# Seven products on quarters in place of eight for the second FFN product, in three of its four parts

## The chip, the core and the metric

The kernel is one program on one NeuronCore of a Trainium2 chip. The metric is the device time of one execution in microseconds (us), taken as the median of several runs. Its engines are TensorE (PE in the profile; PEld is its weight load), VectorE (DVE), ScalarE (ACT), GpSimd (POOL) and SyncE (SP). Sixteen DMA engines move the data. SP starts plain loads, POOL starts loads that add to what is already in the on-chip memory.

## What is computed

Two layers, each a mixer block and a feed-forward block (FFN) on a sequence of 512 tokens of width 1024, all in fp32:

```python
for l in range(2):
    h = rms_norm(x, pre_mix_norm[l])
    ...                                   # conv, pooling, gated unit, sparse attention on h @ w_in
    x = x + rms_norm(mix @ w_out[l], post_mix_norm[l])
    h = rms_norm(x, pre_ffn_norm[l])
    f = square(relu(h @ ffn_w1[l]))       # 512x1024 @ 1024x4096
    x = x + rms_norm(f @ ffn_w2[l], post_ffn_norm[l])   # 512x4096 @ 4096x1024
```

The change lies in `f @ ffn_w2` and in what feeds it.

## The kernel before, in words

Every fp32 product is done as three fp32r matmuls (`mm3`): each operand is split into a high and a low part, and high x high, high x low and low x high are added up in PSUM. A weight unit is 128 x 1024 words (512 KB). `load` brings it from HBM into a raw buffer `wr` (six of them) through SP's queue; `split` makes the high part `wh` on ACT and the low part `wl` on DVE (five buffers each). Of a raw buffer in use, `more` adds another unit to it with an accumulating DMA from POOL, so that a sum of weights costs no engine but the DMA.

The FFN runs in four parts of 1024 hidden columns. In a part, `square4` is called twice. Each call makes a 512 x 512 block of `h @ ffn_w1` by seven products on quarters (Strassen's scheme, Winograd's form) of 24 matmuls with 256 columns each: the seven forms of h are held in `F`, four weight units are loaded, and four accumulating DMAs make the weight sums. `finish` applies the squared relu to a quarter and splits it into `f` (tiles `f`, `hi`, `lo`). Then `tgroup` runs the second product of the part twice, for the two halves of the 1024 output columns: four weight units, four token tiles, 96 matmuls of 512 columns each. The first half's sums go from PSUM (`pm`) into `y` in SBUF by one addition for each token tile; the second half's stay in four PSUM banks of their own (`own`, tile name `po`) over all four parts. After the last part come the norm (`square`, `post`) and the next layer's norm (`norm_tile`).

The order in which every engine works is not that of the text. The kernel is first recorded (`_Rec.add`), then `order` plays it through with a cost for each instruction, for DMA landing times and for free buffers, and each engine's fixed list follows from that; `shift` moves an instruction's rank. A tile of a pool is given out in the order of the text as far as buffers go. Pools that matter here: `wr` 6, `wp` 5, `sc` (scratch, 128 x 512 words) 9, `big` (8 KB a partition: forms `F`, `f`, `y`, mixer tiles) 12, and eight PSUM banks by tag: `mm` 3, `o` 1, `s` 2, `x` 2.

In the listing all instructions are issued from line 442, so the profile's rows tell them apart by the names of the tiles. The lines that the steps touch are `cost` and `order`, `conv_in`, `square4` (`finish`, `first`, the chain of `more`), `mixer`, `ffn` and `POOLS`.

Of the kernel before, what the change touches and what calls it, by code (L numbers as in the profile page):

```python
# [10 lines left out]
F32 = mybir.dt.float32  # L11
# [3 lines left out]
AF = mybir.ActivationFunctionType  # L15
# [4 lines left out]
P = 128  # L20
# [18 lines left out]
FIRST = (2, 3)  # L39
NBIG, NSC = 12, 9  # L40

# [189 lines left out]
class _Rec:  # L231
# [56 lines left out]
    def cost(self, eng, method, args, kw):  # L288
# [6 lines left out]
        if eng == "tensor":  # L295
            if method == "transpose":
                return 0.107
            dt, m = args[1].dtype, args[1].ix.size
            if out.p0:
                return 0.02  # L300
            if dt == F32:
                return max(4 * (n / 2400 + 0.0025), 0.426 * m / 128 if n < 128 else 0.0)
            if dt == F32R:
                return max((17 * n / 16 + 10) / 2400, 0.109 * m / 128)
            return max(0.025, n / 2400 + 0.0025)
# [21 lines left out]
    def order(self):  # L327
# [43 lines left out]
        while len(seq) < n:  # L371
# [30 lines left out]
            if o[1] == "dma_start":  # L402
                v = o[2][0] if isinstance(o[2][0], _V) else o[2][1]
                dma = max(dma, end + 1.1) + v.pn * v.ix.size * 4 / 360e3
                end = dma + (2.0 if e == "sync" else 4.0)
            for t in o[5]:
# [37 lines left out]

POST, FORM, FORM2, FORM3, C11 = -1000, -1000, 0, 500, 500


class _Net:
# [81 lines left out]
    def split_psum(self, hi, lo, ps, scale=None):  # L530
# [4 lines left out]
        else:  # L535
            self.act(hi, ps, AF.Copy, scale=scale)
            self.stt(lo, ps, scale, hi.bitcast(F32), ALU.mult, ALU.subtract)

    def grow(self, l, c0, n):
        t = self.gpool.tile([P, n], F32, name=self.nm("gb"), tag=f"gb{n}", bufs=2)  # L540
        r = self.a["rows"]
        self.nc.sync.dma_start(t, bass.AP(tensor=r.tensor, offset=r.offset + l * r.shape[1] + c0,
                                          ap=[[0, P], [1, n]]))
        return t
# [49 lines left out]
    def norm_forms(self, t, g, forms, tag="x"):  # L594
# [20 lines left out]
        def put(i, v):  # L615
            hi, lo = F[i][:, :, c:c + P], F[i][:, :, 256 + c:256 + c + P]
            self.split_psum(hi, lo, v)
# [9 lines left out]
        r0, r1 = raw[t - 2, 0], raw[t - 2, 1]  # L627
        s3, s1 = four("hs"), four("hs")
        self.act(s1, pts[1])
        self.tt(s1, s1, pts[0], ALU.subtract)  # L630
        put(3, s1)
        self.tt(s3, r0, pts[0], ALU.subtract)
        self.stt(r0, s1, -1.0, r0, ALU.mult, ALU.subtract)
        put(4, r0)
        self.nc.shift = FORM3
        put(5, s3)
        self.stt(r1, r0, -1.0, r1, ALU.mult, ALU.subtract)
# [85 lines left out]
    def conv_in(self, pv, pg, b):  # L723
        th = self.scr("th")
        self.act(th, pg, AF.Tanh, scale=0.5)
        h = self.mp.tile([P, 30 + S], F32, name=self.nm("ch"), tag="ch", bufs=2)
        self.nc.gpsimd.memset(h[:, :30], 0.0)
        self.stt(h[:, 30:], th, 1.0, pv, ALU.add, ALU.mult)
        return h
# [204 lines left out]
    def cmp_probs(self):  # L934
# [13 lines left out]
        self.tt(pc, pc, self.cmask[:, :, None, :].to_broadcast([P, NT, 4, 32]), ALU.add)  # L948
        st = self.mp.tile([P, 3, NT, 4], F32, name=self.nm("cst"), tag="cst", bufs=1)
        nc.vector.tensor_reduce(st[:, 0], pc, AX.X, ALU.max)  # L950
# [9 lines left out]
    def attn_tile(self, i, mix):  # L960
# [64 lines left out]
        nc.tensor.transpose(pt, self.pc[:, i].rearrange("p h n -> p (h n)"), self.ident)  # L1025
        th = self.mp.tile([P, P], F32, name=self.nm("pch"), tag="pch", bufs=1)
        self.act(th, pt)
# [121 lines left out]
    def new_norm(self, l, c0):  # L1149

        return self.grow(l, c0, D), self.new_hT()

    def square4(self, l, u, f, F, early=None):

# [20 lines left out]

        def out(bh, th):
            o = (slice(None), slice(2 * bh, 2 * bh + 2), slice(256 * th, 256 * th + 256))
            return f[0][o], f[1][o]

        def finish(c, op, bh, th):  # L1180
            hi, lo = out(bh, th)
            self.stt(c, c, 0.0, c, op, ALU.mult)
            self.act(hi, c)
            self.tt(lo, c, hi.bitcast(F32), ALU.subtract)

# [5 lines left out]
        def first():  # L1191
            w21 = self.split(self.load(l, u + 1))
            product(a, w21, A12)
            r = view(self.scr("fr"))
            hi, lo = out(0, 0)
            self.nc.shift = C11 if early is not None else 0
            self.act(r, a, AF.Relu)
            self.act(hi, r, AF.Square)
            self.tt(r, r, r, ALU.mult)
            self.tt(lo, r, hi.bitcast(F32), ALU.subtract)  # L1200
            self.nc.shift = 0
# [10 lines left out]
        if early is not None:  # L1212
            first()
            yield
        more(B11, 2)
        B12 = self.load(l, u + 2)
        more(B12, 3)
        t1 = self.split(B11)
        x = bank()
        product(x, t1, S1, True)  # L1220
        c = snap("c", x)
        more(B11, 3)
        t2 = self.split(B11)
        z = bank("o")
        product(z, t2, S2, True)
        add(s1, z)
        add(c, s1)
        more(B11, 1)
        if early is None:
            first()  # L1230
        t3 = self.split(B12)
        y = bank()
        product(y, t3, S3, True)
        add(c, y)
        finish(c, ALU.min, 1, 1)
        w22 = self.split(self.load(l, u + 3))
        product(x, w22, S4)
        c = view(self.scr("c"))
        self.tt(c, s1, x, ALU.add)
        finish(c, ALU.min, 1, 0)  # L1240
        t4 = self.split(B11)
        product(y, t4, A22)
# [4 lines left out]
    def mixer(self, l, norm):  # L1247
# [9 lines left out]
        self.KH, self.KL = K[:, 0:2], K[:, 2:4]  # L1257
        self.V = self.mp.tile([P, NT, P], F32, name=self.nm("V"), tag="V")
        self.Vc = self.mp.tile([P, 2, P], F32, name=self.nm("Vc"), tag="Vc")
        self.Kc = self.mp.tile([P, 64], F32R, name=self.nm("Kc"), tag="Kc")  # L1260
        st = {}

        def mixt():
            t = self.big("mixT")
            return t[:, 0:2], t[:, 2:4]
# [44 lines left out]
        def cout():  # L1310
            st["conv"] = mixt()
            self.conv_out(st["acc"], st["conv"])

        for name in ORDER:
# [5 lines left out]
        m = [(st[n][0][:, c], st[n][1][:, c]) for n in ("nsa", "pool", "sgu", "conv") for c in range(2)]  # L1320
        g = self.grow(l, 1024, D)
        ssv = self.small.tile([P, NT, 2], F32, name=self.nm("ssv"), tag="ssv", bufs=2)
# [3 lines left out]
        places = [self.big("wa") for _ in range(2)]  # L1326
        after = self.grow(l, 2048, D), self.new_forms()
        for dh in range(2):
# [17 lines left out]
    def ffn(self, l, norm):  # L1346
        (g, (F, _)), y = norm
        g2 = self.grow(l, 3072, D)
        after = None
        ssv = self.small.tile([P, NT, 2], F32, name=self.nm("ssv"), tag="ssv", bufs=2)  # L1350

        own = [self.pst([P, 512], "po", "x" if t < 2 else "s") for t in range(NT)]
        u0, n = U_FF, PART
        for part in range(NPART):
            f = [[self.big("f") for _ in range(2)] for _ in range(2)]
            both = [self.square4(l, u0 + 4 * i, (f[0][i], f[1][i]), F, y[:, i] if part == 0 else None)
                    for i in range(2)]
            if part == 0:
                for _ in range(2):
                    for s in both:  # L1360
                        next(s)
            for s in both:
                for _ in s:
                    pass
            u0 += n
            srcs = [(f[0][k // 4][:, k % 4], f[1][k // 4][:, k % 4]) for k in range(n)]
            end = part == NPART - 1
            for t, ps in self.tgroup(lambda j: self.unit(l, u0 + j), srcs, 2):
                yt = y[:, t]
                if part == 0:  # L1370
                    self.act(yt, ps)
                    continue
                self.tt(yt, ps, yt, ALU.add)
                if end:
                    self.square(yt, ssv[:, t, 0:1])
                    self.tt(yt, yt, g2[:, 0:512], ALU.mult)
            u0 += n // 2
            if end and l + 1 < L:
                after = self.new_norm(l + 1, 0)
            for t, ps in self.tgroup(lambda j: self.unit(l, u0 + j), srcs, n // 2 if end else 2, own, part == 0, end):  # L1380
                if not end:
                    continue
                yt = self.scr("yg")
                self.square(ps, ssv[:, t, 1:2], yt)
                self.tt(yt, ps, g2[:, 512:], ALU.mult)
                self.post(t, [y[:, t], yt], ssv[:, t])
                if after:
                    self.norm_tile(t, *after)
            u0 += n // 2
        return after  # L1390

    POOLS = (("cp", 1), ("small", 2), ("par", 1), ("gp", 2), ("sc", NSC), ("wp", 5), ("wr", 6), ("mp", 1),
             ("big", NBIG), ("psum", 2))

# [78 lines left out]
```

## Time and profile before

| | us |
|---|---|
| median of three runs (lowest, highest) | 1073.33 (1072.13, 1074.9) |
| the profiled execution, its own time | 1071.21 |
| its span, first to last instruction | 1069.5 |
| PE busy in the span | 1054.3 |
| DVE busy | 726.1 |
| ACT busy | 505.9 |
| POOL busy | 92.6 |
| time of the DMA packets, share of 16 engines | 28.5% from SP's queue, 19.2% from POOL's |

The profile is of one execution. A row of a group of instructions gives the engine, the operation, the tiles (out<-in), the shape, the count, the busy time, the mean duration of one in ns, and then the idle time of that engine before them with what ended it. Matmuls are pipelined, so the duration of one is longer than the distance from one to the next; distances are read from the chain of work. FFN parts begin where the chain goes over to tile `pf` (the first product).

### The profile page before, as it was taken

The numbers are of one execution on the slowest core, as the hardware profiler recorded it, in microseconds if no ns is written. First come the engines' busy times: TensorE is split into PE (matmuls) and PEld (weight loads), VectorE is DVE, ScalarE is ACT, GpSimd is POOL, SyncE is SP. The second block draws the span as 40 slices with busy tenths as digits, with TensorE's granted clock in tenths as the row PEclk, the third lists the DMA queues.
The fourth block names the chain that finished last, engine by engine and source line by source line (L and its number), as shares of the span: only waits on it lengthen the run. The fifth ranks groups of instructions, "written<-read, shape, count | busy, mean of one in ns | idle before, by whom it ended". The sixth has DMA issues, their size and how long they took to land.

```text
span 1069.5 us, 16960 instructions
## 1 busy us (share of the span) xinstructions
PE 1054.3 (99%) x6850; PEld 920.6 (86%) x6850; DVE 726.1 (68%) x1118; ACT 505.9 (47%) x893; POOL 92.6 (9%) x144
## 2 busy tenths in 40 slices
PE   8999999999999999999999999999999999999997
PEld 6998777898898898898899986788989988988986
DVE  7799876895276366277669998669924753752773
ACT  5437774763252253154444487648423523532531
POOL 3000001200100100100000000111000000001000
PEclk9999999999999999999999999999999999999999
DMA  9330216456566566467144111344665655656512
GB/s 338 106 120 21 79 43 154 110 131 202 119 177 177 97 180 187 91 154 231 38 131 137 60 54 42 64 119 118 178 144 115 175 165 131 172 162 137 155 46 79
DMA packets 39265, 137.44 MB, mean 129 GB/s; under 512 B 4753, under 2 KB 5649, under 8 KB 38930
## 3 DMA queue, kind: packets, MB, share of 16 engines
q1 hardware_dynamic: 29970, 102.79, 28.5%
q0 software_dynamic: 9216, 33.56, 19.2%
q8 instruction: 54, 0.88, 0.3%
q14 instruction: 25, 0.20, 0.1%
HBM read 134.23 MB, written 2.10 MB: 127 GB/s over the span
## 4 chain that ended last, share of the span: by engine, by line
PE 84%; DVE 12%; issue 1%; ACT 1%; POOL 1%; DMA 0%; DVEq 0%; POOLq 0%; SPq 0%; ACTq 0%
PE pf L442 28%; PE pm L442 23%; PE po L442 16%; PE pp L442 6%; PE pc L442 3%; DVE wl L442 3%; DVE cacc L442 2%; PE s L442 2%; PE O L442 2%; PE ppt L442 2%; PE pt L442 1%; DVE h L442 1%; DVE pw L442 1%; DVE xb L442 1%; DVE hs L442 0%
## 5 line engine op out<-in xcount | busy, mean ns | idle before, releaser
L442 DVE TENSOR_TENSOR wl<-wr,wh 128x1024 fp32r<-128x1024 f32 (+1 forms) x220 | 262.4, 1203 | 176.2 <-ACT wh L442 174.3
L442 ACT ACTIVATE wh<-wr 128x1024 fp32r<-128x1024 f32 (+1 forms) x222 | 227.9, 1042 | 275.8 <-DMA wr<-wst 89.6
L442 PE MATMUL pf<-hF,wh 128*128 128x256 f32 x1728 | 300.1, 278 | 1.4 <-DVE hF L442 0.8
L442 PEld LDWEIGHTS pf<-hF,wh 128*128 128x128 f32 x1728 | 262.5, 188 | 4.1 <-DVE hF L442 1.2
L442 PE MATMUL pf<-hF,wl 128*128 128x256 f32 x864 | 238.4, 278 | 0.1
L442 PEld LDWEIGHTS pf<-hF,wl 128*128 128x128 f32 x864 | 162.4, 188 | 1.7 <-DVE wl L442 0.8
L442 PE MATMUL pm<-wh,f 128*128 128x512 f32 x512 | 163.3, 395 | 0.0
L442 PE MATMUL po<-wh,f 128*128 128x512 f32 x512 | 160.5, 392 | 0.0
L442 PEld LDWEIGHTS pm<-wh,f 128*128 128x128 f32 x512 | 96.2, 188 | 23.5 <-DVE c L442 1.8
L442 PEld LDWEIGHTS po<-wh,f 128*128 128x128 f32 x512 | 96.2, 188 | 20.5
L442 POOL DMA_DIRECT2D wr<-wst x64 | 55.4, 866 | 560.1 <-DVE wl L442 404.1
L442 PE MATMUL po<-wl,f 128*128 128x512 f32 x256 | 100.5, 392 | 0.0
L442 PE MATMUL pm<-wl,f 128*128 128x512 f32 x256 | 100.2, 391 | 0.0
L442 PE MATMUL pp<-wh,hT 128*128 128x256 f32 (+1 forms) x512 | 100.2, 289 | 0.0
L442 DVE SCALAR_TENSOR_TENSOR cacc<-ch,cwh,cacc 128x512 f32<-128x512 f32 x120 | 85.1, 742 | 0.5
L442 PE MATMUL pm<-wh,mixT 128*128 128x512 f32 x256 | 83.7, 403 | 0.1
L442 PEld LDWEIGHTS pp<-wh,hT 128*128 128x128 f32 x512 | 80.0, 189 | 0.6
L442 PE MATMUL pp<-wl,hT 128*128 128x256 f32 (+1 forms) x256 | 73.6, 287 | 0.0
L442 PEld LDWEIGHTS pm<-wh,mixT 128*128 128x128 f32 x256 | 47.7, 189 | 12.1 <-issue 1.0
L442 PEld LDWEIGHTS po<-wl,f 128*128 128x128 f32 x256 | 48.1, 188 | 10.8
L442 PEld LDWEIGHTS pm<-wl,f 128*128 128x128 f32 x256 | 48.1, 188 | 9.3
L442 PE MATMUL pm<-wl,mixT 128*128 128x512 f32 x128 | 50.4, 396 | 0.0
(236 smaller groups left out, 1378.4 us busy)
## 6 DMA issues: line engine op xcount, KB each, us to landing
wr<-wst SPq DMA_DIRECT2D x170, 512.0 KB, 4.3
wr<-wst POOLq DMA_DIRECT2D x64, 512.0 KB, 5.8
gb<-rows SPq DMA_DIRECT2D x7, 512.0 KB, 4.9
wr<-wq SPq DMA_DIRECT2D x8, 268.0 KB, 4.6
xres<-x SPq DMA_DIRECT2D x4, 512.0 KB, 5.9
cw<-cw SPq DMA_DIRECT2D x2, 1024.0 KB, 8.1
out<-xres SPq DMA_DIRECT2D x3, 512.0 KB, 2.6
sgw<-sgw SPq DMA_DIRECT2D x2, 256.0 KB, 5.3
```

The source lines that it names most:

```text
L442: getattr(getattr(nc, e), method)(*[real(x) for x in args], **{k: real(x) for k, x in kw.items()})
```

## The change

In parts 0 to 2 the second product (512 x 1024 times 1024 x 1024) is done by seven products on quarters too: 256 tokens x 512 hidden columns times 512 x 512 weights, 24 matmuls of 512 columns each. `square4` no longer splits its result itself but hands each quarter to `emit`, which builds the left-hand forms A11, S3, A12, S1, S2, S4 and A22 (tile names as in `form`), each split in a high and a low part. The weight sums for p5, p7, p6 and q4 are made by accumulating DMAs on raw buffers, two chains of them starting from unit 0 and unit 4. Two of the products (p1 and p7) stay in two PSUM banks each over the three parts; the other five are added up in SBUF (`acc`), by ACT copies in part 0 and DVE additions in parts 1 and 2. In part 3 fourteen DVE additions join them to the output quarters, and part 3's own second product is done as before and added to these.

Beside it: inside `square4` the chain of weight sums starts from B12 and the products come in another order; two of the four quarters get relu and square on ACT; the norm gains come as pairs in a `big` tile; conv input, values and small attention tiles of the mixer lie in one `big` tile `rest`; `big` has 14 buffers; the planner's costs for matmuls of at most 256 columns and for accumulating DMAs are other ones, and the final sums and the conv output get shifts of their own.

```diff
-NBIG, NSC = 12, 9
+NBIG, NSC = 14, 9
...
+                dma = max(dma, end + 1.1) + v.pn * v.ix.size * 4 / (360e3 if e == "sync" else 180e3)
+                end = dma + 2.0
...
+SUMS, CONV, POST, FORM, FORM2, FORM3, C11 = 300, -300, -1000, -1000, 0, 500, 500
+TAGS = "mm", "o"
+FIN = (1, 1), (1, 0)
...
+    def gains(self, *rows):
+        t = self.big("gb", F32).rearrange("p a b -> p (a b)")
+        r = self.a["rows"]
+        out = [t[:, i * D:i * D + D] for i in range(2)]
+        for v, (l, c0) in zip(out, rows):
+            self.nc.sync.dma_start(v, bass.AP(tensor=r.tensor, offset=r.offset + l * r.shape[1] + c0,
+                                              ap=[[0, P], [1, D]]))
+        return out
...
-        h = self.mp.tile([P, 30 + S], F32, name=self.nm("ch"), tag="ch", bufs=2)
+        h = self.rest[:, 542 * b:542 * b + 542]
...
-            hi, lo = out(bh, th)
-            self.stt(c, c, 0.0, c, op, ALU.mult)
-            self.act(hi, c)
-            self.tt(lo, c, hi.bitcast(F32), ALU.subtract)
+            if (bh, th) in FIN:
+                self.act(c, c, AF.Relu, scale=1.0 if op == ALU.max else -1.0)
+                self.act(c, c, AF.Square)
+            else:
+                self.stt(c, c, 0.0, c, op, ALU.mult)
+            emit(bh, th, c)
...
-        more(B11, 2)
         B12 = self.load(l, u + 2)
         more(B12, 3)
+        more(B11, 2)
+        t3 = self.split(B12)
+        y = bank()
+        product(y, t3, S3, True)
         t1 = self.split(B11)
         x = bank()
         product(x, t1, S1, True)
         c = snap("c", x)
-        more(B11, 3)
-        t2 = self.split(B11)
+        add(c, y)
+        more(B12, 0)
+        if early is None:
+            first()
+        t2 = self.split(B12)
         z = bank("o")
         product(z, t2, S2, True)
         add(s1, z)
         add(c, s1)
-        more(B11, 1)
-        if early is None:
-            first()
-        t3 = self.split(B12)
-        y = bank()
-        product(y, t3, S3, True)
-        add(c, y)
         finish(c, ALU.min, 1, 1)
+        more(B12, 1)
         w22 = self.split(self.load(l, u + 3))
         product(x, w22, S4)
         c = view(self.scr("c"))
         self.tt(c, s1, x, ALU.add)
         finish(c, ALU.min, 1, 0)
-        t4 = self.split(B11)
+        t4 = self.split(B12)
...
+        self.rest = self.big("rest", F32).rearrange("p a b -> p (a b)")
+        self.V = self.rest[:, 1084:1596].rearrange("p (t c) -> p t c", t=NT)
+        self.Vc = self.rest[:, 1596:1852].rearrange("p (t c) -> p t c", t=2)
...
+        accs = [y, self.big("acc", F32), self.big("acc", F32)]
+        acc = {"q4": accs[0][:, 0:2], "p2": accs[0][:, 2:4], "p5": accs[1][:, 0:2], "p6": accs[1][:, 2:4],
+               "p3": accs[2][:, 0:2]}
+        own = {"p1": [self.pst([P, 512], "po", "x") for _ in range(2)],
+               "p7": [self.pst([P, 512], "po", "s") for _ in range(2)]}
+        u0 = U_FF
+        for part in range(NPART - 1):
+            uw = u0 + PART
+            form, raw = {}, {}
+            def put(name, bh, v):
+                if name not in form:
+                    form[name] = self.big(name)
+                o = slice(2 * bh, 2 * bh + 2)
+                hi = form[name][:, o, :256]
+                self.act(hi, v)
+                self.tt(form[name][:, o, 256:], v, hi.bitcast(F32), ALU.subtract)
+            def emit0(bh, th, v):
+                raw["A21" if th else "A11", bh] = v
+                if not th:
+                    put("A11", bh, v)
+                if ("A11", bh) in raw and ("A21", bh) in raw:
+                    s3 = self.scr("s3").rearrange("p (b q) -> p b q", b=2)
+                    self.tt(s3, raw["A11", bh], raw["A21", bh], ALU.subtract)
+                    put("S3", bh, s3)
+            def emit1(bh, th, v):
+                raw["A22" if th else "A12", bh] = v
+                if not th:
+                    put("A12", bh, v)
+                if ("A12", bh) in raw and ("A22", bh) in raw:
+                    a11, a21, a12, a22 = (raw[n, bh] for n in ("A11", "A21", "A12", "A22"))
+                    self.tt(a21, a22, a21, ALU.subtract)
+                    put("S1", bh, a21)
+                    self.stt(a11, a21, -1.0, a11, ALU.mult, ALU.subtract)
+                    put("S2", bh, a11)
+                    self.stt(a12, a11, -1.0, a12, ALU.mult, ALU.subtract)
+                    put("S4", bh, a12)
+                    put("A22", bh, a22)
+            def banks():
+                return [self.pst([P, 512], "pm", TAGS[i]) for i in range(2)]
+            def product(pss, units, a, first=True, final=True):
+                for u in range(2):
+                    wh, wl = units(u)
+                    for t in range(2):
+                        c = slice(P * t, P * t + P)
+                        d = slice(256 + P * t, 256 + P * t + P)
+                        for kk in range(2):
+                            k = 2 * u + kk
+                            o = slice(512 * kk, 512 * kk + 512)
+                            self.mm3(pss[t], a[:, k, c], a[:, k, d], wh[:, o], wl[:, o], first and k == 0,
+                                     final and k == 3)
+            def add_up(name, pss):
+                for i in range(2):
+                    v = acc[name][:, i]
+                    if part == 0:
+                        self.act(v, pss[i])
+                    else:
+                        self.tt(v, pss[i], v, ALU.add)
+            more = lambda x, i: self.nc.gpsimd.dma_start(x, self.a["wst"][l, i], accum_op=ALU.add)
+            sq = [self.square4(l, u0 + 4 * i, F, e, y[:, i] if part == 0 else None)
+                  for i, e in enumerate((emit0, emit1))]
...
             if part == 0:
                 for _ in range(2):
+                    for v in sq:
+                        next(v)
+            for _ in sq[0]:
+                pass
+            raws = {}
+            simple = lambda i: lambda j: self.split(self.load(l, uw + i + j))
+            def weights(first, j, *steps):
+                if (first, j) not in raws:
+                    raws[first, j] = self.load(l, uw + first + j)
+                x = raws[first, j]
+                for i in steps:
+                    more(x, uw + i + j)
+                return self.split(x)
+            steps = {"p1": simple(0), "p2": simple(2), "p3": simple(6), "p5": lambda j: weights(0, j, 4),
+                     "p7": lambda j: weights(4, j, 6), "p6": lambda j: weights(4, j, 0),
+                     "q4": lambda j: weights(4, j, 2)}
+            left = {"p1": "A11", "p7": "S3", "p2": "A12", "p5": "S1", "p6": "S2", "p3": "S4", "q4": "A22"}
+            for name in ["p1", "", "p7", "p2", "p5", "p6", "p3", "q4"]:
+                if not name:
+                    for _ in sq[1]:
+                        pass
+                elif name in own:
+                    product(own[name], steps[name], form[left[name]], part == 0, part == NPART - 2)
+                else:
+                    ps = banks()
+                    product(ps, steps[name], form[left[name]])
+                    add_up(name, ps)
+            u0 += 2 * PART
+        plus = lambda v, w: self.tt(v, w, v, ALU.add)
+        f = [[self.big("f") for _ in range(2)] for _ in range(2)]
+        def emit(i):
+            def put(bh, th, v):
+                o = slice(None), slice(2 * bh, 2 * bh + 2), slice(256 * th, 256 * th + 256)
+                self.act(f[0][i][o], v)
+                self.tt(f[1][i][o], v, f[0][i][o].bitcast(F32), ALU.subtract)
+            return put
+        ys = {}
+        self.nc.shift = SUMS
+        for i in range(2):
+            y11, y12, y21, U, w = (acc[n][:, i] for n in ("p2", "p3", "q4", "p6", "p5"))
+            plus(U, own["p1"][i])
+            plus(y11, own["p1"][i])
+            plus(w, U)
+            plus(y21, U)
+            plus(y12, w)
+            plus(w, own["p7"][i])
+            plus(y21, own["p7"][i])
+            ys[i, 0], ys[i, 1], ys[2 + i, 0], ys[2 + i, 1] = y11, y12, y21, w
...
+        g2, g0 = self.gains(*[(l, 3072), (l + 1, 0)][:1 + (l + 1 < L)])
+        uw = u0 + PART
+        for t, ps in self.tgroup(lambda j: self.unit(l, uw + j), srcs, 2):
+            v = ys[t, 0]
+            plus(v, ps)
+            self.square(v, ssv[:, t, 0:1])
+            self.tt(v, v, g2[:, 0:512], ALU.mult)
+        after = (g0, self.new_hT()) if l + 1 < L else None
+        for t, ps in self.tgroup(lambda j: self.unit(l, uw + 4 + j), srcs, 4, own["p1"] + own["p7"]):
+            v = ys[t, 1]
+            self.nc.shift = POST
+            self.tt(v, ps, v, ALU.subtract)
+            self.square(v, ssv[:, t, 1:2])
+            self.nc.shift = 0
+            self.tt(v, v, g2[:, 512:], ALU.mult)
+            self.post(t, [ys[t, 0], v], ssv[:, t])
+            if after:
+                self.norm_tile(t, *after)
```

## Rows read from the trace of the kernel before

**Rows 1.** The page, busy time by engine and the slices' DVE, DMA lines.
```profile
PE 1054.3 (99%) x6850; PEld 920.6 (86%) x6850; DVE 726.1 (68%) x1118; ACT 505.9 (47%) x893; POOL 92.6 (9%) x144
...
DVE  7799876895276366277669998669924753752773
...
DMA  9330216456566566467144111344665655656512
```

**Rows 2.** Stages: window, length; busy PE, PEld, DVE, ACT, POOL; clock, DMA share.
```profile
0.00:207.00 207.00, 201.32 (x1338) 167.82 (x1339) 169.39 (x335) 124.22 (x278) 23.77 (x56) 1.00 0.39 118
...
289.72:372.16 82.44, 82.44 (x530) 74.07 (x530) 45.37 (x53) 30.63 (x36) 6.86 (x8) 1.00 0.62 154
372.16:454.49 82.33, 82.33 (x530) 73.97 (x530) 45.35 (x53) 30.62 (x36) 6.87 (x8) 1.00 0.61 153
454.49:545.00 90.51, 90.51 (x587) 81.59 (x587) 64.51 (x86) 44.24 (x73) 6.59 (x12) 1.00 0.48 137
545.00:735.00 190.00, 188.84 (x1295) 158.66 (x1295) 155.86 (x291) 111.25 (x256) 13.31 (x19) 1.00 0.31 86
```

**Rows 3.** Chain of work, 285 to 380 us: start, length, what, number of instructions.
```profile
289.72 35.39 PE pf L442 x312
...
350.18 21.98 PE po L442 x96
```

**Rows 4.** Groups of instructions in part 1 of layer 0 (289.72 to 372.16 us).
```profile
L442 DVE TENSOR_TENSOR wl<-wr,wh 128x1024 fp32r<-128x1024 f32 x23 | 27.8, 1222 | 25.2 <-ACT wh L442 25.2
L442 ACT ACTIVATE wh<-wr 128x1024 fp32r<-128x1024 f32 x22 | 22.8, 1055 | 38.5 <-DMA wr<-wst 14.6 <-PE pm L442 10.5 <-PE pf L442 10.4
...
L442 DVE TENSOR_TENSOR y<-pm,y 128x512 f32<-128x512 f32 x4 | 2.8, 690 | 4.5 <-PE pm L442 4.5
...
L442 DVE SCALAR_TENSOR_TENSOR c<-c 128x512 f32<-128x512 f32 x4 | 2.7, 688 | 0.1
L442 DVE TENSOR_TENSOR f<-c,f 128x512 fp32r<-128x512 f32 x4 | 2.7, 687 | 0.7 <-ACT f L442 0.7
L442 ACT ACTIVATE f<-c 128x512 fp32r<-128x512 f32 x4 | 2.5, 634 | 6.3 <-DVE c L442 6.3
```

**Rows 5.** DMA queues in the same window: packets, MB, share; issues, us to landing.
```profile
q0 software_dynamic: 1156, 4.21, 31.5%
q1 hardware_dynamic: 2304, 8.39, 29.6%
...
wr<-wst SPq DMA_DIRECT2D x16, 512.0 KB, 4.8
wr<-wst POOLq DMA_DIRECT2D x8, 512.0 KB, 6.0
```

**Rows 6.** DMA queues, 355 to 360 us, accumulating loads alone.
```profile
q0 software_dynamic: 234, 0.89, 104.4%
```

**Rows 7.** DMA queues, 317 to 319 us, plain loads alone.
```profile
q1 hardware_dynamic: 225, 0.83, 103.0%
```

**Rows 8.** DMA queues, 343 to 345 us, both at once.
```profile
q0 software_dynamic: 59, 0.21, 53.3%
q1 hardware_dynamic: 85, 0.34, 46.9%
```

**Rows 9.** POOL in order of time: start, length, instruction, idle before and releaser.
```profile
301.04 0.86 POOL L442 DMA_DIRECT2D wr<-wst  x1 [12.76 <-DVE wl L442]
311.40 0.84 POOL L442 DMA_DIRECT2D wr<-wst  x1 [9.50 <-DVE wl L442]
321.24 0.87 POOL L442 DMA_DIRECT2D wr<-wst  x1 [9.00 <-DVE wl L442]
```

**Rows 10.** What SP's queue waited for, 285 to 375 us.
```profile
SPq L442 <- DVE wl L442: 98.4, 18, 21.6
```

**Rows 11.** All engines in order of time, the end of the program.
```profile
1062.65 0.40 PE L442 MATMUL po<-wh,f 128*128 128x512 f32 x1
1063.08 0.60 ACT L442 ACTIVATE yg<-po 128x512 f32<-128x512 f32 x1 [4.81 <-PE po L442]
...
1063.93 0.68 DVE L442 TENSOR_TENSOR yg<-po,gb 128x512 f32<-128x512 f32 x1
```

More of the change, by code (lines that the diff above doesn't have):

```diff
@@ L303, in cost @@
             if dt == F32R:
-                return max((17 * n / 16 + 10) / 2400, 0.109 * m / 128)
+                return max(((17 if n > 256 else 16) * n / 16 + (6 if n > 256 else 18)) / 2400, 0.109 * m / 128)
             return max(0.025, n / 2400 + 0.0025)
@@ L403, in order @@
                 v = o[2][0] if isinstance(o[2][0], _V) else o[2][1]
-                dma = max(dma, end + 1.1) + v.pn * v.ix.size * 4 / 360e3
-                end = dma + (2.0 if e == "sync" else 4.0)
+                dma = max(dma, end + 1.1) + v.pn * v.ix.size * 4 / (360e3 if e == "sync" else 180e3)
+                end = dma + 2.0
             for t in o[5]:
@@ L442, in issue @@
             getattr(getattr(nc, e), method)(*[real(x) for x in args], **{k: real(x) for k, x in kw.items()})
-POST, FORM, FORM2, FORM3, C11 = -1000, -1000, 0, 500, 500
+SUMS, CONV, POST, FORM, FORM2, FORM3, C11 = 300, -300, -1000, -1000, 0, 500, 500
+TAGS = "mm", "o"
+FIN = (1, 1), (1, 0)
 class _Net:
@@ L628, in norm_forms @@
         s3, s1 = four("hs"), four("hs")
+        self.tt(s3, r0, pts[0], ALU.subtract)
+        put(5, s3)
         self.act(s1, pts[1])
@@ L631, in norm_forms @@
         put(3, s1)
-        self.tt(s3, r0, pts[0], ALU.subtract)
         self.stt(r0, s1, -1.0, r0, ALU.mult, ALU.subtract)
@@ L635, in norm_forms @@
         self.nc.shift = FORM3
-        put(5, s3)
         self.stt(r1, r0, -1.0, r1, ALU.mult, ALU.subtract)
@@ L948, in cmp_probs @@
         self.tt(pc, pc, self.cmask[:, :, None, :].to_broadcast([P, NT, 4, 32]), ALU.add)
-        st = self.mp.tile([P, 3, NT, 4], F32, name=self.nm("cst"), tag="cst", bufs=1)
+        st = self.rest[:, 1980:2028].rearrange("p (a t h) -> p a t h", a=3, t=NT)
         nc.vector.tensor_reduce(st[:, 0], pc, AX.X, ALU.max)
@@ L1025, in attn_tile @@
         nc.tensor.transpose(pt, self.pc[:, i].rearrange("p h n -> p (h n)"), self.ident)
-        th = self.mp.tile([P, P], F32, name=self.nm("pch"), tag="pch", bufs=1)
+        th = self.rest[:, 1852:1980]
         self.act(th, pt)
@@ L1149, in new_norm, with square4 @@
     def new_norm(self, l, c0):
-        return self.grow(l, c0, D), self.new_hT()
-    def square4(self, l, u, f, F, early=None):
+        return None, self.new_hT()
+    def square4(self, l, u, F, emit, early=None):
         A11, A12, A22, S1, S2, S3, S4 = F
@@ L1174, in snap @@
             return v
-        def out(bh, th):
-            o = (slice(None), slice(2 * bh, 2 * bh + 2), slice(256 * th, 256 * th + 256))
-            return f[0][o], f[1][o]
         def finish(c, op, bh, th):
-            hi, lo = out(bh, th)
-            self.stt(c, c, 0.0, c, op, ALU.mult)
-            self.act(hi, c)
-            self.tt(lo, c, hi.bitcast(F32), ALU.subtract)
+            if (bh, th) in FIN:
[4 more added lines that the diff above has]
+            emit(bh, th, c)
         bank = lambda tag="mm": self.pst([P, 2, 256], "pf", tag)
@@ L1194, in first @@
             r = view(self.scr("fr"))
-            hi, lo = out(0, 0)
             self.nc.shift = C11 if early is not None else 0
             self.act(r, a, AF.Relu)
-            self.act(hi, r, AF.Square)
-            self.tt(r, r, r, ALU.mult)
-            self.tt(lo, r, hi.bitcast(F32), ALU.subtract)
+            self.act(r, r, AF.Square)
+            emit(0, 0, r)
             self.nc.shift = 0
@@ L1257, in mixer @@
         self.KH, self.KL = K[:, 0:2], K[:, 2:4]
-        self.V = self.mp.tile([P, NT, P], F32, name=self.nm("V"), tag="V")
-        self.Vc = self.mp.tile([P, 2, P], F32, name=self.nm("Vc"), tag="Vc")
+        self.rest = self.big("rest", F32).rearrange("p a b -> p (a b)")
+        self.V = self.rest[:, 1084:1596].rearrange("p (t c) -> p t c", t=NT)
+        self.Vc = self.rest[:, 1596:1852].rearrange("p (t c) -> p t c", t=2)
         self.Kc = self.mp.tile([P, 64], F32R, name=self.nm("Kc"), tag="Kc")
@@ L1311, in cout @@
             st["conv"] = mixt()
+            self.nc.shift = CONV
             self.conv_out(st["acc"], st["conv"])
+            self.nc.shift = 0
         for name in ORDER:
@@ L1320, in mixer @@
         m = [(st[n][0][:, c], st[n][1][:, c]) for n in ("nsa", "pool", "sgu", "conv") for c in range(2)]
-        g = self.grow(l, 1024, D)
+        g, g1 = self.gains((l, 1024), (l, 2048))
         ssv = self.small.tile([P, NT, 2], F32, name=self.nm("ssv"), tag="ssv", bufs=2)
@@ L1326, in mixer @@
         places = [self.big("wa") for _ in range(2)]
-        after = self.grow(l, 2048, D), self.new_forms()
+        after = g1, self.new_forms()
         for dh in range(2):
@@ L1346, in ffn @@
     def ffn(self, l, norm):
-        (g, (F, _)), y = norm
-        g2 = self.grow(l, 3072, D)
-        after = None
+        (_, (F, _)), y = norm
         ssv = self.small.tile([P, NT, 2], F32, name=self.nm("ssv"), tag="ssv", bufs=2)
[L1352 to L1357, printed above, removed]
+        accs = [y, self.big("acc", F32), self.big("acc", F32)]
@@ L1358, in ffn @@
             if part == 0:
                 for _ in range(2):
[L1360 to L1388, printed above, removed]
@@ L1389, in ffn @@
-            u0 += n // 2
-        return after
-    POOLS = (("cp", 1), ("small", 2), ("par", 1), ("gp", 2), ("sc", NSC), ("wp", 5), ("wr", 6), ("mp", 1),
-             ("big", NBIG), ("psum", 2))
+                    for v in sq:
[11 more added lines that the diff above has]
+                return self.split(x)
@@ new lines, in ffn @@
+        self.nc.shift = 0
+        for i in range(2):
+            for _ in self.square4(l, u0 + 4 * i, F, emit(i)):
+                pass
+        srcs = [(f[0][k // 4][:, k % 4], f[1][k // 4][:, k % 4]) for k in range(PART)]
+        g2, g0 = self.gains(*[(l, 3072), (l + 1, 0)][:1 + (l + 1 < L)])
[5 more added lines that the diff above has]
+            self.tt(v, v, g2[:, 0:512], ALU.mult)
@@ new lines, in ffn @@
+        after = (g0, self.new_hT()) if l + 1 < L else None
[4 more added lines that the diff above has]
+            self.square(v, ssv[:, t, 1:2])
+            self.nc.shift = 0
+            self.tt(v, v, g2[:, 512:], ALU.mult)
+            self.post(t, [ys[t, 0], v], ssv[:, t])
+            if after:
+                self.norm_tile(t, *after)
@@ L1395, in run @@
+        return after
+    POOLS = (("cp", 1), ("small", 2), ("par", 1), ("gp", 2), ("big", NBIG), ("sc", NSC), ("wp", 5), ("wr", 6),
+             ("mp", 1), ("psum", 2))
     def run(self):
```

## The prediction

> **What bounds the kernel now.** I read the page first: PE is busy 1054.3 us of a span of 1069.5, the others much less [rows 1]. That alone proves little, because a matmul's row is longer than its pitch; so next comes the table by stages. The middle FFN parts take 82.44 and 82.33 us and PE is busy in all of it, while DVE has 45.37, ACT 30.63 and POOL 6.86 us of work there and the DMA share is 0.62 [rows 2]. Then the chain of work: in such a part it is PE alone, 312 matmuls of 256 columns in 35.39 us and 96 of 512 columns in 21.98 us [rows 3], so the pitches are 113.4 ns and 229.0 ns. A part has 336 of the first and 192 of the second: 38.1 + 44.0 = 82.1 us. The part's time is PE's pitch to within 0.3 us; nothing else is late. A matmul fewer is worth its full pitch as long as its weights, forms and banks come in time. That is the question of this case.
>
> **What is removed.** In three parts of each layer the second product goes from 192 to 7 x 24 = 168 matmuls of 512 columns. 24 x 0.229 = 5.50 us a part, six parts: 33.0 us. The first product keeps its 336. A changed part is 38.1 + 38.5 = 76.6 us of PE.
>
> **What is added to DVE and ACT in a changed part.** Splits: seven products take two units each, 14 in place of 8, so 28 with the first product's 14 (the window shows 22 or 23 [rows 4]). Quarter-size DVE operations (128 x 512, 0.688 us by the rows of `y`, `c` and `f` [rows 4]): 10 additions and 2 squarings in `square4`, 8 differences for the forms, 14 low parts, 10 additions into `acc`: 44, where there were 30. DVE: 28 x 1.222 + 44 x 0.688 = 64.5 us; the same count of before (22 and 30) gives 47.5 where the window shows 45.37, as neighbouring rows overlap, so 62 to 64.5 of 76.6 us, some 82%. ACT: 28 x 1.055 + 30 x 0.62 (two snapshots, four more for the FIN quarters, two for the first quarter, per call, and 14 high parts) = 48 us, 63%. Part 0 puts the 10 additions on ACT. All of this lies beside PE: it costs nothing while a weight's split can be done ahead. The five `wp` buffers let splits run up to four units of 2.7 us, some 11 us, ahead of PE, and the forms have cover too: S1 is needed two products (11 us) after the last quarter of the second call, and its way there is about five operations of 0.7 us.
>
> **What is added to the DMA engines.** This is the tight one. The loads of a part go from 16 to 18 (two units for each of p1, p2, p3 and for each of the two chains), the accumulating ones from 8 to 16 (`square4` keeps its 8). The part now gives q0 31.5% and q1 29.6% of 82.44 us [rows 5]: 3.25 us of all 16 engines for an accumulating load and 1.53 us for a plain one. Where the engines were full the price was lower: 0.89 MB in 5 us of accumulating alone [rows 6] is 2.95 us for one, and 0.83 MB in 2 us of plain loads [rows 7] is 1.26 us. So a changed part needs between 18 x 1.26 + 16 x 2.95 = 69.9 us and 18 x 1.53 + 16 x 3.25 = 79.5 us of DMA engine time, where PE needs 76.6: 91 to 104%. Before it was 61%. POOL's issuing, 16 x 0.86 = 14 us, is no limit.
>
> The two queues do not add capacity: with both in work at 343 to 345 us they had 53.3% and 46.9%, together 100% [rows 8]. The Trainium skill says so too ("DMA: Bandwidth & Descriptors", section "Rules for kernel authors": spreading transfers over the issuing engines doesn't help, as all run on the same 16 engines), and by that rule the DMA rival below stands; the trace agrees. The same page (section "Anatomy of one DMA") fits a transfer from POOL at 2.0 us plus its bytes over 436 GB/s; an estimate by it is 3.2 us for one and 34 x 1.2 = 41 us of engine time a part, which would leave no DMA rival. The trace differs: 6.0 us to landing [rows 5] and 2.95 to 3.25 us of engine time for an accumulating load, so the rows decide.
>
> What of this ends on the path? The least is 0.0 us a part (69.9 fits under 76.6), and engines busy without a hole at the high price give 79.5 - 76.6 = 2.9 us. Little can be taken ahead: only six raw buffers exist, the waits of SP's queue for a split to free one add up to 98.4 us within 285 to 375 us [rows 10], and the second product's two chains hold two of them from p7 to q4. I take the middle, 1.45 us a part, 8.7 us for six parts.
>
> **The chains of weight sums.** Now one step of a chain takes about 10 us (accumulating loads at 301.04, 311.40, 321.24, each waiting for a split before it [rows 9]). In the new `square4` two steps lie between the splits for S3 and for A22, 20 us, and PE has five products (13.6 us) between them plus the lead of the splits, 11 us: it just fits. In the second product p7, p6 and q4 hang on one chain, with 11 to 16 us of other products between them: it fits. I cost both at nothing beyond the DMA term; the cover is the 11 us of lead. Gone, each `square4` would lose up to 20 - 13.6 = 6 us.
>
> **Banks.** Four products a part take their second tile in the single `o` bank that the product before has just filled. Its addition is 0.69 us behind a DVE that may be in a split (up to 1.22 us), against six matmuls of the other tile (1.37 us) as cover: 0 to 0.55 us each, at most 13 us in 24 turns. I take 0, as the second unit's six matmuls for the first tile can stand in front too.
>
> **Ends and moves.** At each layer's end the output half is now a DVE subtraction from PSUM first, 0.68 us, then the square; before, the square read PSUM straight (0.60 us, 0.4 us after PE's last matmul began) and the DVE product lay beside it [rows 11]. At the program's end this is on the path: +0.7 us, +0.8 with the handover. In layer 0 the next mixer's matmuls cover it (PE is busy 90.51 of 90.51 us there [rows 2]); without them it would cost 0.8 too. The fourteen final additions a layer, 9.6 us of DVE, have the two first products of part 3 (38 us) as cover; late they would hold up the last 96 matmuls, which need those banks, by at most the 9.6. The mixers run in another order and with shared tiles; PE is idle there by 5.7 us in layer 0, mostly before the first data, and by 1.2 us in layer 1 [rows 2], so the gain is at most 1 us; for the loss I allow 3, and take 0.
>
> **Sum.** Against the profiled execution's own 1071.2 us: -33.0 + 8.7 + 0.8 = -23.5, so 1047.7. That execution is 2.1 us below the median of the three runs (1073.33). On the median's footing: **1050 us**.
>
> **Rivals.**
> - PE alone still decides. For it: the low DMA price, and PE's idle time of 0.3 us a part today. Against it: 91% is already near the top for six buffers. Time: 1073.3 - 33.0 + 0.8 = 1041.
> - The DMA engines decide at the high price, never idle: 79.5 us a part, or the same loss through the `o` bank. -33.0 + 17.4 + 0.8: 1058.5; with both, up to 1071. For it: the mean prices of the part. Against it: those means were taken at a share of 0.6, and full stretches were cheaper.
> - Slower: the DMA engines decide and also stand idle, since a chain's next load starts only after DVE has read the raw buffer. At the high price a part passes today's 82.4 us when the engines are idle over 3.5% of it (79.5/82.4 is 0.965). Idle 8% of the time, the price is 79.5/0.92 = 86.4, +4.0 us a part: 1073.3 + 24 + 0.8 = 1098; at 5%, 1081. For it: the waits in rows 9 and 10. Against it: five split units stand between DMA and PE, and POOL and SP queues rarely both wait.
>
> **How the numbers follow.** Chances: the forecast (1045 to 1055) 0.43, PE alone (below 1045) 0.25, DMA without holes (1055 to 1070) 0.19, slower 0.09, and 0.04 for what lies between. A measurement of this kernel can tell about 0.3% (3.2 us) from no change. Faster 0.87, the same 0.04, slower 0.09. The range goes from 1040, PE alone with nothing lost, to 1070, DMA at the high price with the bank turns; it leaves 0.15 out.
>
> **What would show it.** Right: 144 matmuls fewer of 512 columns; changed parts of 77 to 79 us; DMA share in them 0.9 or more; DVE around 62 us; PE's idle time in them released by `wl` or `wh`, which themselves waited for `wr` from the DMA; the tail after PE's last matmul longer by 0.8 us. Wrong: a DMA share under 0.85 with PE full (the accumulating loads got cheaper still, and it is PE alone); idle time of PE released by forms, `acc` or `f` tiles (DVE decides, which I hold off the path); or a mixer that is longer by more than 3 us.

## The result and the profile after

The changed kernel takes 1055.33 us in the median of four runs (1053.45 to 1058.26), the kernel before 1073.05: ratio 0.9835, 95% interval 0.9809 to 0.9862. The forecast was 1050 with a range of 1040 to 1070. The profiled execution took 1053.45 us, its span is 1051.7.

The page: busy time by engine, and the slices' DMA line. PE has 144 matmuls fewer than in [rows 1], DVE 99 us and ACT 105 us more work, and the DMA engines stand at 8 to 9 tenths in the changed parts.

```profile
PE 1024.9 (97%) x6706; PEld 891.7 (85%) x6706; DVE 824.8 (78%) x1250; ACT 611.0 (58%) x1057; POOL 137.6 (13%) x192
...
DMA  8330244379989899986034110534998989989802
```

The stages of the kernel after (window, length, busy time of PE, PEld, DVE, ACT, POOL, clock, DMA share, GB/s): layer 0 with its mixer, parts 0, 1, 2, and part 2 of layer 1.

```profile
0.00:207.00 207.00, 200.73 (x1342) 167.79 (x1343) 170.04 (x336) 125.39 (x279) 22.30 (x52) 1.00 0.38 116
207.00:282.44 75.44, 75.34 (x482) 67.00 (x481) 62.09 (x81) 52.55 (x77) 13.54 (x15) 1.00 0.87 213
282.44:363.01 80.57, 78.35 (x506) 69.11 (x505) 60.12 (x72) 45.85 (x59) 14.28 (x17) 1.00 0.89 222
363.01:443.84 80.83, 78.03 (x507) 69.30 (x506) 66.00 (x82) 44.80 (x58) 14.85 (x18) 1.00 0.93 224
...
881.01:961.67 80.66, 78.02 (x506) 69.32 (x506) 65.13 (x81) 45.19 (x59) 14.46 (x17) 1.00 0.94 224
```

Parts 1 and 2, 82.44 and 82.33 us before [rows 2], give only 1.9 and 1.5 us. By the pitches a changed part is 76.6 us of PE, so each loses about 4 us; 2.2 to 2.8 us of that PE is seen idle, the rest lies between matmuls whose rows still touch. Part 0, where ACT empties the five products' banks, shows no loss: PE is busy in 75.34 of its 75.44 us. Parts 1 and 2 are longer than the 77 to 79 us that the prediction named as its sign.

What PE waited for in the whole kernel after (us in total, times, longest), the lines of tile `pm`:

```profile
PE pm L442 <- DVE acc L442: 4.1, 4, 1.4
PE pm L442 <- DVE wl L442: 3.3, 4, 1.0
...
PE pm L442 <- DVE y L442: 1.7, 4, 0.6
...
PE pm L442 <- ACT wh L442: 1.1, 4, 0.3
PE pm L442 <- DVE S L442: 0.6, 2, 0.3
```

`pm` is also the name of the mixer's output product, and 1.2 us of the 1.7 for `y` are the mixer's, two of the four times. Of the page's groups:

```profile
L442 PE MATMUL pm<-wh,mixT 128*128 128x512 f32 x256 | 84.0, 401 | 1.2 <-DVE y L442 1.2
```

So in the second product PE waits 4.1 + 0.5 = 4.6 us for banks to be emptied, and 3.3 + 1.1 + 0.6 = 5.0 us for splits and forms.

And in order of time, PE's interrupted rows of part 1 (start, length, instruction, idle time before and its releaser), 339 to 352 us:

```profile
339.82 0.50 PE L442 MATMUL pm<-wh,S 128*128 128x512 f32 x1 [0.21 <-ACT wh L442]
340.59 0.50 PE L442 MATMUL pm<-wh,S 128*128 128x512 f32 x1 [0.27 <-DVE y L442]
341.72 0.50 PE L442 MATMUL pm<-wl,S 128*128 128x512 f32 x1 [0.63 <-DVE wl L442]
351.49 0.50 PE L442 MATMUL pm<-wh,S 128*128 128x512 f32 x1 [0.78 <-DVE acc L442]
```

Two kinds of releaser stand here. `acc` and `y` are the additions that empty a PSUM bank. `wl`, `wh` and `S` are splits and forms; the chain of work of the same stretch shows DVE alone for 10 us, almost without a gap, from the last quarter of the first product to the split that PE waits for (some of its pieces; the last three are PE's next products, interrupted by an addition that empties a bank):

```profile
331.36 0.70 DVE s L442
...
333.98 1.13 DVE wl L442
335.12 0.60 DVE S L442
...
336.32 0.60 DVE y L442
...
340.53 1.14 DVE wl L442
...
341.72 9.00 PE pm L442 x38
...
350.74 0.70 DVE acc L442
...
351.49 11.52 PE pm L442 x48
```

In part 2 a DMA stands in the chain as well:

```profile
423.76 8.60 DMA wr<-wst
```

So three causes are on the table: late accumulating loads (theory A, the forecast's extra term), the single `o` bank of the five products (theory B, which the forecast put at 0), and DVE's pile of work at the end of the second call of `square4` (theory C).

### The profile page after: what moved, and what is told of

Same layout as the page of the kernel before. It is cut to its first block, busy times and chain, and to the rows that moved or that the text cites. A ratio compares the mean times of both kernels' runs of the same rounds, so it can differ in the third digit from the quotient of the medians.

```text
span 1051.7 us, 17150 instructions
## 1 busy us (share of the span) xinstructions
PE 1024.9 (97%) x6706; PEld 891.7 (85%) x6706; DVE 824.8 (78%) x1250; ACT 611.0 (58%) x1057; POOL 137.6 (13%) x192
## 4 chain that ended last, share of the span: by engine, by line
PE 74%; DVE 11%; DMA 7%; issue 5%; ACT 3%; POOL 1%; POOLq 0%; DVEq 0%; SPq 0%; ACTq 0%
PE pf L442 24%; PE pm L442 22%; PE po L442 8%; PE pp L442 6%; DMA wr<-wst 6%; PE pc L442 3%; PE O L442 2%; PE s L442 2%; DVE wl L442 2%; PE ppt L442 2%; DVE cacc L442 2%; ACT wh L442 1%; PE pt L442 1%; POOL r L442 1%; PE ph L442 1%
## 5 line engine op out<-in xcount | busy, mean ns | idle before, releaser
L442 DVE TENSOR_TENSOR wl<-wr,wh 128x1024 fp32r<-128x1024 f32 (+1 forms) x256 | 305.0, 1205 | 95.1 <-ACT wh L442 93.8
L442 POOL DMA_DIRECT2D wr<-wst x112 | 97.0, 900 | 511.6 <-DVE wl L442 255.2
L442 PE MATMUL pm<-wh,S 128*128 128x512 f32 x288 | 95.1, 400 | 6.5 <-DVE acc L442 4.1
L442 DVE SCALAR_TENSOR_TENSOR cacc<-rest,cwh,cacc 128x512 f32<-128x512 f32 x120 | 85.9, 742 | 0.4
L442 PEld LDWEIGHTS pm<-wh,S 128*128 128x128 f32 x288 | 53.8, 188 | 25.3 <-DVE acc L442 6.7
L442 PE MATMUL pm<-wh,A 128*128 128x512 f32 x192 | 63.0, 395 | 0.0
L442 PE MATMUL pm<-wl,S 128*128 128x512 f32 x144 | 56.7, 396 | 3.3 <-DVE wl L442 3.3
L442 ACT ACTIVATE c<-c 128x512 f32<-128x512 f32 x64 | 37.8, 622 | 24.7 <-DVE c L442 24.4
L442 PEld LDWEIGHTS pp<-wl,hT 128*128 128x128 f32 x256 | 48.2, 188 | 0.3
L442 PE MATMUL pc<-hT,wh 128*128 128x256 f32 x256 | 47.4, 287 | 0.8 <-ACT hT L442 0.8
```

Source lines behind the costliest of these rows:

```text
L442: getattr(getattr(nc, e), method)(*[real(x) for x in args], **{k: real(x) for k, x in kw.items()})
```

## The experiments

All times are medians; the ratio is against runs of the kernel before on the same chip.

**banks.** The changed kernel, with p5 and p3 in two `mm` banks, so that no two products in a row want `o`.

```diff
-            def banks():
-                return [self.pst([P, 512], "pm", TAGS[i]) for i in range(2)]
+            def banks(tags=TAGS):
+                return [self.pst([P, 512], "pm", t) for t in tags]
-                    ps = banks()
+                    ps = banks(("mm", "mm") if name in ("p5", "p3") else TAGS)
```

> The changed kernel (1055.3 us) with one edit: products p5 and p3 take two mm banks in place of one mm and the single o bank, so that no two products in a row want o; the order is planned anew. If the turn of the o bank is what holds PE in parts 1 and 2 (theory B): 6 to 8 us less, 1047 to 1049, and PE's waits for acc and y go. If DVE's pile of work after the second call of the first product is (theory C): 0 to 2 us less. If late accumulating loads are (theory A, the forecast's): within 1 us of 1055.

1041.03 us, ratio 0.9694 (0.9673 to 0.9716): 14.3 us less than the change, about twice what theory B expected (15 us by the two ratios, 12.2 by the spans of the two profiled executions). The stages of parts 1 and 2:

```profile
283.14:360.80 77.66, 77.66 (x511) 70.26 (x511) 58.63 (x71) 45.63 (x59) 13.27 (x16) 1.00 0.94 227
360.80:438.88 78.08, 77.11 (x502) 69.05 (x501) 64.23 (x80) 44.88 (x58) 13.76 (x16) 1.00 0.94 228
```

80.57 and 80.83 became 77.66 and 78.08 us with about the same work on DVE (58.63 and 64.23 us, where it was 60.12 and 66.00) and ACT, and a DMA share that rose to 0.94. In layer 1 the same two parts went from 81.39 and 80.66 to 77.52 and 78.09 us. The four parts together give 12.1 of the 12.2 us between the two spans, so the loss lay in them, and part 0 has no share in it. PE's waits for `acc` are gone, and the 1.2 us for `y` that are left are the mixer's:

```profile
PE pm L442 <- DVE y L442: 1.2, 2, 0.6
```

**banks_late.** The same, and S4 and A22, needed last, get a later rank.

```diff
+                    self.nc.shift = 200
                     put("S4", bh, a12)
                     put("A22", bh, a22)
+                    self.nc.shift = 0
```

> The same bank edit, and the forms S4 and A22, which are needed last, get a later rank (+200) so that DVE does the splits of weights before them; planned anew. Theory B: as the bank edit alone, 1047 to 1049. Theory C: 4 to 6 us below the bank edit alone. Both at work: 1043 to 1046. Theory A: 1054 to 1056.

1039.47 us, ratio 0.9671 (0.965 to 0.9693). 1.6 us below the bank edit, less than theory C alone wanted (4 to 6), and the two intervals overlap, so a gain by the rank is not shown. It is the fastest version of this study that leaves nothing out.

**x_dma.** The changed kernel's order kept; the second product's 48 accumulating loads (marked when they are recorded) cut to 128 columns after the order is made.

```diff
+    for i in rec.marked:
+        x, src = rec.ops[i][2]
+        rec.ops[i][2] = (x[:, :128], src[:, :128])
```

> The changed kernel's own order of all instructions kept, but the 48 accumulating loads of the second product move 128 of 1024 columns each (so those weight sums are left out for the other columns): DMA time falls by about 8 x 2.7 = 22 us a changed part. Theory A: the 4 us a part that parts 1 and 2 lose come back, 12 to 16 us less, 1039 to 1043. Theories B and C: only the wait for a load that stands in part 2 goes, 2 to 4 us less, 1051 to 1053.

1050.31 us, ratio 0.9777 (0.9762 to 0.9793): 5.0 us less (2.8 by the spans of the profiled executions). Theory A wanted 12 to 16, theories B and C 2 to 4; the median lies outside both, nearer to the second. In layer 0 part 1 still takes 80.50 us and part 2 80.06, at a DMA share of only 0.73 and 0.76, so the load on the DMA engines is not what keeps these parts at 80 us. The DMA piece of part 2 is gone from the chain of work, and DVE's pile stands in its place; the end of part 2 looks like part 1:

```profile
419.89 0.60 DVE S L445
...
422.81 1.23 DVE wl L445
...
424.08 20.16 PE pm L445 x86
```

**x_act.** The order kept; the ten additions of a part (marked likewise, in parts 1 and 2) go to ACT as copies.

```diff
+    for i in rec.marked:
+        o = rec.ops[i]
+        o[0], o[1], o[2], o[3] = "scalar", "activation", (o[2][0], o[2][1], AF.Copy), {}
```

> The changed kernel's own order kept, but in parts 1 and 2 the ten additions of a product into acc are ACT copies out of PSUM (so the sum over parts is left out), as they are in part 0. Takes 10 x 0.6 us of DVE a part away, and the o bank is emptied by an engine with less queued. Theories B and C: 8 to 12 us less, 1043 to 1047. Theory A: within 2 us of 1055.

1055.72 us, ratio 0.9831 (0.9803 to 0.9858): nothing. This is a miss of B and C together. DVE has 4.5 us less work in each of the two parts (55.59 in place of 60.12, 61.52 in place of 66.00), and the parts are as long as before:

```profile
282.74:363.59 80.85, 78.38 (x505) 69.11 (x505) 55.59 (x63) 50.25 (x68) 14.69 (x17) 1.00 0.91 223
363.59:444.45 80.86, 78.62 (x506) 69.23 (x506) 61.52 (x74) 49.78 (x68) 14.63 (x17) 1.00 0.93 222
```

PE's waits for emptied banks in the second product are as long too, 4.2 us for `acc` and 0.5 for `y`, now ended by ACT. So neither DVE's amount of work nor the engine that empties the bank is, in this order, what costs the 4 us. What the run shares with the change is the order. PE's list for the start of p5 in part 1 of the two kernels, with the number of matmuls in a row (from the recorded order, no time in it):

```
change:  p5 first tile 1, p6 first tile 7, p3 first tile 1, p5 second tile (o) 1, p5 first tile 5, p5 second tile 5, p6 first tile 5, p3 first tile 6, ...
banks:   p5 first tile 2, p5 second tile 2, p5 first tile 4, p5 second tile 4, p6 first tile 6, p6 second tile (o) 6, ...
```

With `o` still taken by p2, the planner fills PE with p6 and p3. These need S2, S4 and their weights' splits, so DVE and ACT make three products' forms and splits ahead of the second half of p5's. That the pile on DVE is the bank's doing is read from these two lists; no run shows it by itself.

**act_new.** ACT copies in all parts, and the order planned anew.

```diff
-                    if part == 0:
-                        self.act(v, pss[i])
-                    else:
-                        self.tt(v, pss[i], v, ALU.add)
+                    self.act(v, pss[i])
```

> The changed kernel with ACT copies in place of DVE additions into acc in all parts (the sum over parts is left out), this time planned anew. If the run with the order kept gained nothing because the order itself carries the wait for the bank: part of the loss comes back, 1048 to 1052 (still one o bank, so not 1041). If the engine that empties the bank makes no difference at all: 1054 to 1057.

1049.78 us, ratio 0.9778 (0.9753 to 0.9803): 5.5 us less. The same edit that gives nothing in the old order gives over a third of the bank edit's gain in a new one. So part of the loss is carried by the order. It is not shown that running later products early is what costs it: the recorded order of act_new runs p6 and p3 ahead of p5's second half too, and so does that of part 0, which loses nothing. How much of the loss is the wait at the bank and how much the late splits stays open. Whether the bank edit in the old order would give anything was not tried: in that order the first tiles of p5, p6 and p3 hold all three `mm` banks.

**banks_mm.** All five products in `mm` banks, planned anew.

```diff
-                    ps = banks()
+                    ps = banks(("mm", "mm"))
```

> The changed kernel with both tiles of all five products in mm banks (three of them), none in o; planned anew. Theory B: the turn moves to the three mm banks, of which two are always taken and the third is wanted at once by the next product and by the first product's accumulations: between the bank edit (1041) and the change (1055.3), 1043 to 1050. If it were only the o bank as such and not the number of free banks: 1039 to 1042.

1047.48 us, ratio 0.9767 (0.9752 to 0.9782), between the two as theory B had it. This fits the number of banks free at a product's start as the cause, and speaks against `o` as such. `o` then stands empty between the first product's turns, and waits for emptied banks are back (`acc`, and 1.8 of the 2.9 us for `y`; the rest is the mixer's):

```profile
PE pm L442 <- DVE y L442: 2.9, 4, 1.0
...
PE pm L442 <- ACT acc L442: 1.4, 2, 0.7
```

**late_dma.** The fastest version, with the accumulating loads of the second product cut as in x_dma.

> The version with two mm banks for p5 and p3 and the later rank of S4 and A22 (1039.5 us), its 48 accumulating loads of the second product cut to 128 of 1024 columns, planned as before the cut (those weight sums are left out for the other columns). Theory A (with the banks mended the DMA engines, 0.92 to 0.95 busy, are the next limit): 4 to 8 us less, 1031 to 1035. Theory B (at that load they still hide behind PE): 0 to 2 us less, 1037 to 1040.

1038.74 us, ratio 0.9686 (0.9672 to 0.9699), where the uncut version has 1039.47 and 0.9671: no difference. The DMA share of parts 1 and 2 falls from 0.92 and 0.93 to 0.75 and 0.73, and PE, full in both, does not notice. Part 1 of the uncut version, then a window of about the same part of the cut one:

```profile
282.21:360.25 78.04, 78.04 (x506) 70.96 (x506) 60.20 (x72) 45.72 (x60) 13.87 (x16) 1.00 0.92 224
```

```profile
282.00:360.00 78.00, 78.00 (x505) 70.93 (x505) 59.24 (x71) 46.79 (x62) 13.88 (x16) 1.00 0.75 183
```

**others.** The changed kernel with the second product put back; all other edits stay.

> The changed kernel with the second product put back to 192 matmuls in all four parts; what stays is the rest of the change: the new order and chain in the first product, relu and square of two quarters on ACT, gains and small mixer tiles in big tiles, 14 big buffers, the planner's costs and shifts. Theory B (all of the shortfall is in the second product's banks): within 3 us of the kernel before, 1071 to 1075, as the forecast had it. Theory D (the other edits bring something of their own, which hid a part of the loss): 4 to 8 us below the kernel before, 1066 to 1070.

1071.61 us, ratio 0.9994 (0.9983 to 1.0004): the other edits bring and cost nothing that can be told apart from zero. All of the change's gain is the second product's.

## Why the prediction was right, and where it was not

**What bounds the kernel, and what is removed: right.** 6850 - 144 = 6706 matmuls. Once the banks are free the 33.0 us come, as near as the runs can tell: banks is 33.3 us below the kernel before (30.5 to 35.1 by its interval).

**DVE and ACT: right.** I counted 62 to 64.5 us of DVE and 48 of ACT in a changed part; part 1 shows 60.12 and 45.85, part 2 66.00 and 44.80, so DVE in part 2 is a little above my range. Put on the path at nothing: x_act, with 4.5 us of DVE less and no gain, agrees.

**The DMA term: its work was right, its place on the path wrong.** The queues in part 1 of the kernel after (packets, MB, share of 16 engines):

```profile
q0 software_dynamic: 2308, 8.40, 56.5%
q1 hardware_dynamic: 2592, 9.44, 32.7%
...
wr<-wst SPq DMA_DIRECT2D x18, 512.0 KB, 7.1
wr<-wst POOLq DMA_DIRECT2D x17, 512.0 KB, 7.4
```

Of 80.57 us that is 45.5 us for 16 units' worth of accumulating loads (2.85 us each) and 26.3 for 18 plain ones (1.46 each), 71.9 in all: near the low end of my 69.9 to 79.5. For the middle of the two ends I charged 8.7 us. With PE's order in good shape the right charge is none: late_dma. In the changed kernel's own order cutting the loads gives 5.0 us back, so there it is not none. Loads take longer to land (7.1 and 7.4 us against 4.8 and 6.0 in [rows 5]), but PE does not feel that in the version with the banks mended. The 5.0 us of x_dma go with that order, which asks for three products' weights at once; that this is their reason is argued and not shown. The chains of weight sums that feed the first product, which I put at nothing, cost little: PE waits 1.2 us in all for a split at `pf`. The Trainium skill's fit for a transfer from POOL ("DMA: Bandwidth & Descriptors", section "Anatomy of one DMA"), would, by an estimate of 1.2 us of moving for 512 KB, have given a charge of zero too, with a wrong price: the trace has 2.85.

**The banks: the step that failed.** I bounded the turns of `o` by 13 us and took 0, because "the second unit's six matmuls for the first tile can stand in front too". The measured figure is 14.3 us, near my bound for 24 turns; but it arose in the 16 turns of parts 1 and 2, for which my 0.55 us a turn gives 8.8. The reasoning priced a wait at the bank, and that is the smaller part: in the second product PE's waits for `acc` and `y` add up to 4.6 us. The planner did put other matmuls in front, as I had said, but those of p6 and p3, and what they need was not always ready: PE waits 5.0 us for splits and forms. The rest of the 14.3 us no wait in the profile names. A cover that pulls work forward has a price in the queues that must deliver that work.

**The sum.** 33.0 removed, tail 0.8, and in place of 8.7 for the DMA and 0 for the banks 14.3 for the banks: -17.9, measured -17.7. The 14.3 is itself a difference of two runs, so this sum checks the 33.0 and the 0.8 and not the banks. The 5.0 us of x_dma are not added to it, as they are gone once the banks are mended. That the forecast came within 5.3 us is partly luck: a charge for the DMA engines of 8.7 us, for which the runs show 5.0 in this order and none with the banks mended, stood in for over half of the banks' 14.3, which I had put at nothing.

**Ends and moves: right.** From the last matmul's end to the end of the span: 1044.43 to 1051.7, 7.3 us, against 6.45 before [rows 11], +0.8. The subtraction stands in it:

```profile
1044.46 0.69 DVE L442 TENSOR_TENSOR acc<-po,acc 128x512 f32<-128x512 f32 x1 [1.29 <-PE po L442]
1045.24 0.63 ACT L442 ACTIVATE junk<-acc 128x512 f32<-128x512 f32 x1 [4.78 <-DVE acc L442]
```

The mixer of layer 0 kept its 201 us of PE in 207, and others shows no loss.

**The rivals.** PE alone (1041, 0.25) is what the kernel becomes with two more `mm` turns (1041.03). The measured 1055.33 lies just outside the band of the forecast (1045 to 1055) and in that of the next rival (1055 to 1070, chance 0.19). That rival named two reasons: its DMA engines without holes did not decide, but its "same loss through the `o` bank" is what the runs bear out, at 14.3 us in place of 17.4. The slower case did not come. My own list of what would speak against me had the right line, idle time of PE released by forms and `acc`, with a reading (DVE decides) that x_act does not bear out.

## What to carry to other kernels

Count PSUM banks before engine time: when several products follow each other and one bank in the pair is single, a product cannot begin its second tile until that of the product before it is emptied. Here the planner filled that wait with later products, and the profile showed late splits, forms and loads beside it; another bank for the product was worth more than cutting those. And keep the order when you cheapen a step, then plan anew: a gain in the second run alone points to the order.

## What was unexpected of the hardware

Sixteen DMA engines at a share of 0.92 to 0.95 over whole parts of 77 to 78 us cost TensorE nothing that late_dma could show. An accumulating load took less engine time at the higher load (2.85 us at a share of 0.89 in the kernel after, 2.99 at 0.92 in part 1 of banks_late, against 3.25 at 0.62 in [rows 5]) while its landing came later (7.4 and 7.8 us against 6.0).
